# A decoder block's first stage in a written order, and a sink as a key column

## The chip, the cores and the metric

The kernel runs on one core of a Trainium2 chip. The metric is the device time of one execution in microseconds (us); the time of a kernel is the median of several runs.

## The reference

One residual block on x, 512 tokens by 1024 channels, in float32:

```python
h = rmsnorm(x, norm_mix)                     # x * rsqrt(mean(x*x) + eps) * g
proj = h @ w_in                              # split: qa, ka, va | qb, kc, vc, ksl, vsl, kw, vw, g_nsa | g_a, g_b
y_a = swa_sink_attention(qa, ka, va, sinks, table_a)      # 8 heads of 64, 2 key groups, window 128
y_b = nsa_attention(qb, compress(kc), compress(vc), ksl, vsl, kw, vw, sigmoid(g_nsa), table_b)
merged = sigmoid(g_a) * (y_a @ w_up_a) + sigmoid(g_b) * (y_b @ w_up_b)
x = x + merged @ w_out
u, g = split(causal_dwconv(rmsnorm(x, norm_ffn) @ w_ffn_in))
x = x + (silu(g) * u) @ w_ffn_out
out = rmsnorm(x, norm_final)
```

Of the sliding-window attention these lines matter here. The sink is one more logit for each head, which takes part in the softmax and has no value:

```python
logits = einsum('bqgrd,bkgd->bgrqk', qb, kb) * scale + bias      # bias: a function of query - key
logits = where(valid, logits, NEG)                               # 256 keys for 128 queries, the window is 128
probs = softmax(concatenate([logits, sink_col], axis=-1), axis=-1)[..., :span]
out = einsum('bgrqk,bkgd->bqgrd', probs, vb)
```

## The kernel before

All of it is one function, `hybrid`, in which nested helpers issue the work; the order of an engine's instructions is the order of the code, as a scheduling layer with priorities has arranged it. Products run on TensorE in a 32-bit form with fewer mantissa bits (fp32r). Each operand is therefore split into a high part (a cast on ScalarE, L79) and a low part (source minus high, L80, on VectorE or for weights named in `POOLJ` on GpSimd), and each product is three: high by high, high by low, low by high (`three`, L90).

The first stage takes the four token tiles of x in turn (`norm_x`, L152): squares and their sum on ScalarE (L156), the sum of two halves on VectorE (L158), a power on GpSimd, a scaling by the reciprocal root and the weight row `gam` on VectorE (L161), transposition on TensorE (L144), and the split into `xTh` and `xTl`. `values` (L171) then makes the 408 columns of values and gates of a tile with 24 products of 128x408 on TensorE. The weights `wv` for it come in two halves, `wvr` 0 and 1, each split whole (`wvh`, `wvl`).

After it a generator, `filler` (L213), hands out projections as jobs, named in `AORD` and `GORD`: `p_ka`, `p_qa` four times, `p_kc` and so on, each 24 products of 128x512, each with a weight load on SP's queue. Attention units call for the next piece of a job whenever they would wait. `unit_a` (L475) is one tile of 128 queries of one key group of the sliding window. Its first step makes four score tiles (`scores`, L439): two products, then one VectorE instruction (L449) that adds the bias tile TA, writes Pa and keeps the least value. The sink joins in three VectorE lines (L491, L494, L496) and a fifth exponential. Its second step scales, transposes and multiplies by VA.

The bias tile is made from the table by `pg` (L421, three products with a one-hot matrix `og`), copied back into the second half of `og` on ScalarE (L422), written to DRAM 32 times over as `gdr` (L423), and read back as a Toeplitz tile by `toeplitz` (L426 to L429), for TA in four DMAs of 32 partitions.

Of the kernel before, what the change touches and what calls it, by code (L numbers as in the profile page):

```python
# [6 lines left out]
F32 = mybir.dt.float32  # L7
# [4 lines left out]
P = 128  # L12
# [37 lines left out]
def hybrid(tc, x, wv, wblk, w1, w2, wua, wub, wout, wfi, wfo, nmix, nffn, nfin, sinks, par, table, onehot, out):  # L50
# [9 lines left out]
    with es:  # L60
        C = es.enter_context(tc.tile_pool(name="const", bufs=1))
        SL = es.enter_context(tc.tile_pool(name="slots", bufs=1))
        WR = es.enter_context(tc.tile_pool(name="wring", bufs=3))
        SM = es.enter_context(tc.tile_pool(name="small", bufs=4))
# [12 lines left out]

        def split(hi, lo, src, eng=None):
            A.copy(hi, src)  # L79
            (eng or V).tensor_tensor(lo, src, f(hi), op=ALU.subtract)  # L80
# [22 lines left out]
        for h in range(2):  # L103
            sl = slice(h * 512, (h + 1) * 512)
            nc.sync.dma_start(xt[0][:, sl], x[0:P, sl])
            if h == 0:
                nc.sync.dma_start(grow[:, :D], nmix)
        ones = grow[:, D:]
        V.memset(ones, 1.0)
        gam = [bank("sc", f"gam{h}") for h in range(2)]  # L110
        for h in range(2):
            T.matmul(gam[h], ones, grow[:, h * 512 : (h + 1) * 512], start=True, stop=True)
# [3 lines left out]
        nc.sync.dma_start(wvr[0], wv[0])  # L116
        nc.sync.dma_start(xt[1], x[P : 2 * P])
        nc.sync.dma_start(wvr[1], wv[1])
        for t in range(2, NT):
            nc.sync.dma_start(xt[t], x[t * P : (t + 1) * P])  # L120

        ident = C.tile([P, P], F32, name="ident")
        make_identity(nc, ident)
        mhalf = C.tile([P, 1], F32, name="mhalf")
        V.memset(mhalf, -0.5)
        prm = C.tile([P, par.shape[1]], F32, name="prm")
        nc.sync.dma_start(prm, par)
# [6 lines left out]
        def rstd_of(ssq, name):  # L134
            r = SM.tile([P, 1], F32, tag="rstd", name=f"rstd_{name}")
# [14 lines left out]
        halves = [slice(0, 512), slice(512, 1024)]  # L150

        def norm_x(t):  # L152
            s2 = SM.tile([P, 2], F32, tag="s2", name=f"s2x_{t}")
            for h in range(2):
                junk = bank("o", f"junk{t}{h}")
                A.activation(junk, xt[t][:, halves[h]], AF.Square, accum_out=s2[:, h : h + 1])  # L156
            ssq = SM.tile([P, 1], F32, tag="ssq", name=f"ssq{t}")
            V.tensor_tensor(ssq, s2[:, 0:1], s2[:, 1:2], op=ALU.add)  # L158
            r = rstd_of(ssq, f"n1_{t}")
            for h in range(2):  # L160
                V.scalar_tensor_tensor(xt[t][:, halves[h]], xt[t][:, halves[h]], r, gam[h], op0=ALU.mult, op1=ALU.mult)  # L161
                transposed(xt[t], xTh, xTl, t, h, "x")

# [7 lines left out]
        def values(t):  # L171
            ps = bank("mm", f"v{t}")
            sl = slice(t * P, (t + 1) * P)
            order = [(i, k) for h in range(2) for i in (0, 2) for k in range(4 * h, 4 * h + 4)] + [(1, k) for k in range(KD)]
            for n, (i, k) in enumerate(order):
                h, kk = k // 4, k % 4
                T.matmul(ps[:, :NV], (xh, xh, xl)[i](k)[:, sl], (wvh, wvl, wvh)[i][h][:, kk], start=(n == 0), stop=(n == 23))
# [12 lines left out]
        for h in range(2):  # L190
# [22 lines left out]
        def filler():  # L213
            i, nxt = 0, jobs[0][1]()
            while nxt is not None:
                name, _, run = jobs[i]
                cur, nxt, i = nxt, None, i + 1
                if i < len(jobs):
                    with hp(i >= HPJ):
# [96 lines left out]
        def keys(tile_, c0=0):  # L316
            def evac(ps):
                for g in range(2):
                    src = ps[64 * g : 64 * g + 64]
                    hi, lo = tile_()[:, g, 0, c0 : c0 + S], tile_()[:, g, 1, c0 : c0 + S]  # L320
# [24 lines left out]
        KA = lazy("KA", 6, [P, 2, 2, S])  # L345
# [12 lines left out]
        evacs = dict(kc=blocks_of(0), vc=blocks_of(1), ka=keys(KA), ksl=keys(KS, 32), kw=keys(KW),  # L358
# [47 lines left out]
        nsink = C.tile([P, 8], F32, name="nsink")  # L406
        nc.sync.dma_start(nsink, bc(sinks, 8))
        V.tensor_scalar(nsink, nsink, -1.0, None, op0=ALU.mult)
        tab = C.tile([33, 16], F32, name="tab")
        G.memset(tab, 1.0)  # L410
        nc.sync.dma_start(tab[:32], table)
        og = slot(15, [33, 2, ZA + ZW], F32, "og")
        oh, gsb = og[:, 0], og[:8, 1]
        nc.sync.dma_start(oh, onehot)
# [4 lines left out]
        for c0, c1, h0 in ((0, ZA, 0), (ZA, ZA + 512, 8), (ZA + 512, ZA + ZW, 8)):  # L419
            pg = bank("sc", f"pg{c0}")  # L420
            T.matmul(pg[:8, : c1 - c0], tab[:, h0 : h0 + 8], oh[:, c0:c1], start=True, stop=True)  # L421
            A.copy(gsb[:, c0:c1], pg[:8, : c1 - c0])  # L422
# [12 lines left out]
        TA = slot(10, [P, 8, 256], F32, "TA")  # L435
        toeplitz(TA, 0, 8, 0, 256)

# [37 lines left out]
        def unit_a(b, g):  # L475
            n = P if b == 0 else 256
            c0, y0 = (0, P) if b == 0 else ((b - 1) * P, 0)
            st = {}

            def s1():  # L480
                nm = SM.tile([P, 4], F32, tag="nma", name="nma", bufs=3)
                sm = SM.tile([P, 4], F32, tag="sma", name="sma", bufs=3)
                es_ = SM.tile([P, 4], F32, tag="esa", name="esa", bufs=3)
                pr = []
                for r in range(4):
                    p = AT.tile([P, 512], F32, tag="P", name="Pa", bufs=8)
                    c = scores(p, QA[g](), r, b, KA(), g, c0, n, TA, 4 * g + r, y0, nm[:, r : r + 1])
# [13 lines left out]
            def s2():  # L501
# [22 lines left out]
        def unit_b(b, g, br, st):  # L524
# [4 lines left out]
            def s1():  # L529
                Q, Tt = QB[g](), TB[g]  # L530
                nm = SM.tile([P, 4], F32, tag="nmb", name="nmb")
                sm = SM.tile([P, 4], F32, tag="smb", name="smb")
# [3 lines left out]
                if br == 1:  # L536
                    nc_, sc_ = (SM.tile([P, 4], F32, tag=t_, name=t_) for t_ in ("nmc", "smc"))
# [178 lines left out]
        for t in range(NT):  # L716
# [6 lines left out]
            s2 = SM.tile([P, 2], F32, tag="s2", name=f"s2_{t}")  # L723
# [5 lines left out]
            ssq = SM.tile([P, 1], F32, tag="ssq", name=f"ssq2_{t}")  # L729
# [34 lines left out]
        s2s = [SM.tile([P, 2], F32, tag=f"s3_{t}", name=f"s3_{t}", bufs=1) for t in range(NT)]  # L764
# [9 lines left out]
        for h in range(2):  # L774
# [10 lines left out]
            for t in range(NT):  # L785
# [13 lines left out]
                for c in range(2):  # L799
                    sl = slice(512 + 256 * c, 768 + 256 * c)  # L800
                    V.tensor_tensor(xo[:, sl], xo[:, sl], po[t][:, 256 * c : 256 * c + 256], op=ALU.add)
                    sc = SM.tile([P, 1], F32, tag="ssq", name=f"ssq3_{t}{c}")
                    A.activation(junk[:, sl], xo[:, sl], AF.Square, accum_out=sc)
                    V.scalar_tensor_tensor(ms, sc, 1.0 / D, ms, op0=ALU.mult, op1=ALU.add)
                r = SM.tile([P, 1], F32, tag="rstd", name=f"rstd_n3_{t}")
# [71 lines left out]
```

## Time and profile before

| | us |
|---|---|
| median of 3 runs | 770.8 (770.65 to 771.38) |
| the profiled execution | 771.21 |
| its span | 769.4 |
| TensorE busy | 747.5 (97%) |
| VectorE busy | 451.0 (59%) |
| ScalarE busy | 369.4 (48%) |
| GpSimd busy | 156.8 (20%) |
| mean granted TensorE clock | 0.989 |

The span is the time between the first and the last instruction of the profiled execution. PE is TensorE, DVE is VectorE, ACT is ScalarE, POOL is GpSimd, and SP issues DMAs. An entry `[3.67 <-DVE QB L333]` says how long an engine was idle just before an instruction, and what released it. The line numbers are those of the code above.

### The profile page before, as it was taken

The numbers are of one execution on the slowest core, as the hardware profiler recorded it, in microseconds if no ns is written. First come the engines' busy times: TensorE is split into PE (matmuls) and PEld (weight loads), VectorE is DVE, ScalarE is ACT, GpSimd is POOL, SyncE is SP. The second block draws the span as 40 slices with busy tenths as digits, with TensorE's granted clock in tenths as the row PEclk, the third lists the DMA queues.
The fourth block names the chain that finished last, engine by engine and source line by source line (L and its number), as shares of the span: only waits on it lengthen the run. The fifth ranks groups of instructions, "written<-read, shape, count | busy, mean of one in ns | idle before, by whom it ended". The sixth has DMA issues, their size and how long they took to land.

```text
span 769.4 us, 9745 instructions
## 1 busy us (share of the span) xinstructions
PE 747.5 (97%) x3590; PEld 623.3 (81%) x3590; DVE 451.0 (59%) x921; ACT 369.4 (48%) x692; POOL 156.8 (20%) x134
## 2 busy tenths in 40 slices
PE   7999989999999999999999999999999999999996
PEld 5788778788888888878889888888888888888885
DVE  5537988747655578759465665665556564214123
ACT  7345685745655856665344434343434443113213
POOL 5023536325333444402400000000000000002001
PEclk9999998999999999999999999999999999999999
DMA  8463335421112112405321323232322324232302
GB/s 304 98 148 111 108 93 169 126 83 55 56 55 83 55 60 69 145 1 192 111 78 60 109 83 110 82 110 89 104 92 101 102 90 136 85 107 85 107 28 109
DMA packets 24182, 76.74 MB, mean 100 GB/s; under 512 B 3748, under 2 KB 4900, under 8 KB 24134
## 3 DMA queue, kind: packets, MB, share of 16 engines
q1 hardware_dynamic: 24134, 76.12, 31.2%
q8 instruction: 28, 0.46, 0.3%
q14 instruction: 20, 0.16, 0.1%
HBM read 72.96 MB, written 3.15 MB: 99 GB/s over the span
## 4 chain that ended last, share of the span: by engine, by line
PE 89%; DVE 6%; issue 1%; POOL 1%; ACT 1%; DMA 1%; SPq 0%; POOLq 0%; DVEq 0%; ACTq 0%
PE ug L91 10%; PE ug L92 10%; PE ug L93 10%; PE fo L772 5%; PE fo L771 5%; PE fo L770 5%; PE pT L456 3%; PE up L91 2%; PE p_gb L91 2%; PE p_gb L92 2%; PE p_gb L93 2%; PE up L93 2%; PE up L92 2%; PE wo L91 2%; PE wo L92 2%; PE wo L93 2%
## 5 line engine op out<-in xcount | busy, mean ns | idle before, releaser
L92 PE MATMUL ug<-hTl,hl_fi 128*128 128x512 f32 (+1 forms) x376 | 141.1, 375 | 0.0
L93 PE MATMUL ug<-hTh,hl_fi 128*128 128x512 f32 (+1 forms) x376 | 141.1, 375 | 0.0
L91 PE MATMUL ug<-hTh,hl_fi 128*128 128x512 f32 (+1 forms) x376 | 140.9, 376 | 0.0
L93 PEld LDWEIGHTS ug<-hTh,hl_fi 128*128 128x128 f32 x376 | 70.8, 188 | 12.9
L91 PEld LDWEIGHTS ug<-hTh,hl_fi 128*128 128x128 f32 x376 | 70.6, 188 | 12.9
L92 PEld LDWEIGHTS ug<-hTl,hl_fi 128*128 128x128 f32 x376 | 70.8, 188 | 12.6
L754 ACT ACTIVATE cv<-ug,prm 128x512 f32<-128x512 f32 x44 | 34.3, 780 | 96.2 <-PE ug L93 96.2
L755 DVE SCALAR_TENSOR_TENSOR cv<-ug,prm,cv 128x511 f32<-128x511 f32 x44 | 33.0, 750 | 77.1 <-ACT cv L754 77.0
L771 PE MATMUL fo<-hl_fo,AH 128*128 128x512 f32 x176 | 68.8, 391 | 0.0
L770 PE MATMUL fo<-hl_fo,AH 128*128 128x512 f32 x176 | 67.3, 389 | 0.0
L796 POOL TENSOR_TENSOR X<-X,nfin 128x512 f32<-128x512 f32 x4 | 5.2, 1319 | 297.0 <-ACT junk L794 297.0
L80 DVE TENSOR_TENSOR hl_fo<-raw_fo,hl_fo 128x1024 fp32r<-128x1024 f32 x22 | 27.1, 1235 | 64.7 <-ACT hl_fo L79 64.7
L79 ACT CAST hl_fo<-raw_fo 128x1024 fp32r<-128x1024 f32 x22 | 23.1, 1052 | 65.8 <-PE fo L772 65.8
L80 DVE TENSOR_TENSOR hl_fi<-raw_fi,hl_fi 128x1024 fp32r<-128x1024 f32 x44 | 53.5, 1217 | 1.8 <-ACT hl_fi L79 1.8
L772 PE MATMUL fo<-hl_fo,AL 128*128 128x512 f32 x128 | 49.8, 389 | 0.0
L80 DVE TENSOR_TENSOR ptl<-pT,pth 128x512 fp32r<-128x512 f32 x54 | 36.5, 685 | 19.0 <-ACT pth L79 9.9
L378 ACT ACTIVATE Pb<-Pb,nmb 128x512 f32<-128x512 f32 (+3 forms) x64 | 35.9, 562 | 23.9 <-DVE nmb L449 23.6
L79 ACT CAST hl_fi<-raw_fi 128x1024 fp32r<-128x1024 f32 x44 | 45.5, 1037 | 2.4 <-PE wo L93 2.4
L79 ACT CAST pth<-pT 128x512 fp32r<-128x512 f32 x54 | 30.9, 587 | 17.7 <-PE ob L611 8.2
L771 PEld LDWEIGHTS fo<-hl_fo,AH 128*128 128x128 f32 x176 | 33.0, 188 | 7.2
L770 PEld LDWEIGHTS fo<-hl_fo,AH 128*128 128x128 f32 x176 | 33.0, 188 | 7.1
L449 DVE CUSTOM_DVE_ANT_0 Pb<-scores,TB 128x512 f32<-128x512 f32 (+3 forms) x64 | 30.7, 486 | 11.1 <-PE scores L445 9.2
(313 smaller groups left out, 1730.0 us busy)
## 6 DMA issues: line engine op xcount, KB each, us to landing
raw_fi<-in_wfi_dram SPq DMA_DIRECT2D x44, 512.0 KB, 3.3
raw_fo<-in_wfo_dram SPq DMA_DIRECT2D x22, 512.0 KB, 3.3
raw_w<-in_w_dram SPq DMA_DIRECT2D x8, 512.0 KB, 3.8
raw_ga<-in_wblk_dram SPq DMA_DIRECT2D x8, 512.0 KB, 3.3
raw_gb<-in_wblk_dram SPq DMA_DIRECT2D x8, 512.0 KB, 3.2
raw_wo<-in_wout_dram SPq DMA_DIRECT2D x5, 512.0 KB, 3.9
raw_qa<-in_wblk_dram SPq DMA_DIRECT2D x4, 512.0 KB, 4.9
raw_qb<-in_wblk_dram SPq DMA_DIRECT2D x4, 512.0 KB, 6.2
```

The lines of the kernel that those rows point to most:

```text
L79: A.copy(hi, src)
L80: (eng or V).tensor_tensor(lo, src, f(hi), op=ALU.subtract)
L91: T.matmul(ps, wh, xh, start=start, stop=False)
L92: T.matmul(ps, wh, xl, start=False, stop=False)
L93: T.matmul(ps, wl, xh, start=False, stop=stop)
L378: last_exp[0] = A.activation(a[0], a[1], AF.Exp, **k)
L449: V.tensor_tensor_reduce(ptile[:, :n], ps[:, :n], Tt[:, h, y0 : y0 + n], 1.0, HUGE, ALU.add, ALU.min, nm)
L754: A.activation(c, ps, AF.Identity, scale=cw(2, blk), bias=cb(blk))
L755: V.scalar_tensor_tensor(c[:, 1:], ps[:, : S - 1], cw(1, blk), c[:, 1:], op0=ALU.mult, op1=ALU.add)
L770: T.matmul(po[t], ah, wh, start=(k == 0), stop=False)
L771: T.matmul(po[t], ah, wl, start=False, stop=False)
L772: T.matmul(po[t], al, wh, start=False, stop=(k == NF - 1))
```

## The change

Four things are altered. **The first stage** is written out by hand, in a block whose order the scheduling layer keeps. x of tile 1 is loaded before the weights `wv`; the norm's row goes through ScalarE's queue; eight products on a zeroed tile (`busy`) stand ahead of the first work; each half of `wv` is split in two parts, and all low parts are made on GpSimd; the squares of a tile are summed and scaled by two VectorE operations; the products of different tiles are interleaved; the `pg` products and the copies of `og` stand late in the block. Weight loads of the projections are ordered behind the last transposed tile on their engines only. **GpSimd's subtractions** of a split (L80 before, L87 after) are cut into pieces of 256 columns. **The sink** becomes a column of keys: KA has two zero columns ahead of each tile of 128 keys, TA has two columns in its middle, one with the negative sink and one with 1e30, and the scores are 130 or 258 columns wide in place of 128 or 256; the sink's own lines go. TA is read back in two halves, eight DMAs. **The small tiles** are placed before the slots, with fewer buffers and sizes padded.

```diff
         def split(hi, lo, src, eng=None):
-            A.copy(hi, src)
-            (eng or V).tensor_tensor(lo, src, f(hi), op=ALU.subtract)
+            xparts.append(A.copy(hi, src))
+            step = 256 if eng is G else 1 << 20
+            n = hi.shape[-1]
+            for c in range(0, n, step):
+                sl = (slice(None),) * (len(hi.shape) - 1) + (slice(c, min(c + step, n)),)
+                xparts.append((eng or V).tensor_tensor(lo[sl], src[sl], f(hi)[sl], op=ALU.subtract))
...
-        norm_x(0)
-        VA = slot(16, [P, NT, 2, P], F32R, "VA")
-        for h in range(2):
-            split(wvh[h], wvl[h], wvr[h], (G, None)[h])
-        for t in range(1, NT):
-            norm_x(t)
-            values(t - 1)
-        values(NT - 1)
+        with tc.manual_schedule():
...
+            nc.scalar.dma_start(grow[:, :D], nmix)
...
+            busy(5)
...
+            busy(3)
+            squares(0)
+            squares(1)
+            scaled(0, 0)
+            scaled(0, 1)
+            wv_hi(0, 0)
+            x_T(0, 0)
...
+            values_out(1)
+            for c0, c1, h0 in ((0, ZA, 0), (ZA, ZA + 512, 8), (ZA + 512, ZA + ZW, 8)):
+                pg = bank("pt", f"pg{c0}")
+                T.matmul(pg[:8, : c1 - c0], tab[:, h0 : h0 + 8], oh[:, c0:c1], start=True, stop=True)
+                A.copy(gsb[:, c0:c1], pg[:8, : c1 - c0])
+            values(2, 1, (0, 2, 1))
...
         def filler():
-            i, nxt = 0, jobs[0][1]()
+            with tc.issue_after(xlast[0].ins), tc.issue_after(xlast[1].ins):
+                i, nxt = 0, jobs[0][1]()
...
-        TA = slot(10, [P, 8, 256], F32, "TA")
-        toeplitz(TA, 0, 8, 0, 256)
+        TA = slot(10, [P, 2112], F32, "TA")[:, :2064].rearrange("p (h y) -> p h y", h=8)
+        V.tensor_scalar(TA[:, :, P], nsink, -1.0, None, op0=ALU.mult)
+        V.memset(TA[:, :, P + 1], 1e30)
+        toeplitz(TA[:, :, :P], 0, 8, 0, P)
+        toeplitz(TA[:, :, P + 2 :], 0, 8, P, P)
...
-            n = P if b == 0 else 256
-            c0, y0 = (0, P) if b == 0 else ((b - 1) * P, 0)
+            n, nk, y0 = (P + 2, 1, P) if b == 0 else (2 * P + 2, 2, 0)
+            c0 = 0 if b == 0 else (b - 1) * (P + 2) + 2
...
-                ns = nsink[:, 4 * g : 4 * g + 4]
-                V.tensor_tensor(nm, nm, ns, op=ALU.min)
                 for r in range(4):
                     exp(pr[r][:, :n], pr[r][:, :n], bias=nm[:, r : r + 1], scale=-1.0, accum_out=sm[:, r : r + 1])
-                V.tensor_tensor(es_, nm, ns, op=ALU.subtract)
-                exp(es_, es_)
-                V.tensor_tensor(sm, sm, es_, op=ALU.add)
                 V.reciprocal(sm, sm)
```

On VectorE the first rows of the stage move. `ssq` is a tile's sum of squares, `x` the scaled tile, `xTl` its low part. Before, the scaling of the first tile's halves follows its own sum:

```order
L158 TENSOR_TENSOR ssq_120<-s2x_115 128x1
L136 TENSOR_SCALAR rstd_n_0_122<-ssq_120 128x1
L161 SCALAR_TENSOR_TENSOR x_79<-x_79,rstd_n_0_122,gam_85 128x512
L161 SCALAR_TENSOR_TENSOR x_79<-x_79,rstd_n_0_122,gam_86 128x512
L80 TENSOR_TENSOR xTl_111<-tp_x_0_126,xTh_109 128x4x128
L80 TENSOR_TENSOR xTl_112<-tp_x_1_134,xTh_110 128x4x128
```

and after, at the same place:

```order
L158 TENSOR_SCALAR ssq_146<-s2x_141 128x1
L159 TENSOR_SCALAR ssq_146<-s2x_141,ssq_146 128x1
L158 TENSOR_SCALAR ssq_156<-s2x_151 128x1
L159 TENSOR_SCALAR ssq_156<-s2x_151,ssq_156 128x1
L164 SCALAR_TENSOR_TENSOR x_75<-x_75,rstd_n_0_149,gam_131 128x512
L164 SCALAR_TENSOR_TENSOR x_75<-x_75,rstd_n_0_149,gam_132 128x512
L87 TENSOR_TENSOR xTl_92<-tp_x_0_164,xTh_90 128x4x128
```

The sums of the second tile (`ssq_156`) now stand ahead of the scaling of the first.

On ScalarE the middle of the stage has squares (`junk`), weight casts (`wvh`) and the high parts `xTh`. Before:

```order
L79 CAST wvh_91<-wvr_89 128x1632
L79 CAST xTh_109<-tp_x_0_126 128x4x128
L156 ACTIVATE junk_147,s2x_146<-x_79 128x512
L79 CAST xTh_110<-tp_x_1_134 128x4x128
L156 ACTIVATE junk_149,s2x_146<-x_79 128x512
L79 CAST wvh_92<-wvr_90 128x1632
L156 ACTIVATE junk_207,s2x_206<-x_80 128x512
L156 ACTIVATE junk_209,s2x_206<-x_80 128x512
```

and after, from the first part of `wvh`:

```order
L170 CAST wvh_83<-wvr_81 128x816
L81 CAST xTh_90<-tp_x_0_164 128x4x128
L81 CAST xTh_91<-tp_x_1_172 128x4x128
L170 CAST wvh_83<-wvr_81 128x816
L81 CAST xTh_90<-tp_x_0_192 128x4x128
L156 ACTIVATE junk_200,s2x_199<-x_76 128x512
L156 ACTIVATE junk_202,s2x_199<-x_76 128x512
L170 CAST wvh_84<-wvr_82 128x816
L81 CAST xTh_91<-tp_x_1_211 128x4x128
L170 CAST wvh_84<-wvr_82 128x816
```

The squares of the third tile stand between the second tile's first `xTh` and the cast of the second weight half.

Further on, still on ScalarE, are the copies of the bias rows `og`, behind which the write of `gdr` is issued. `hl_ka` and `hl_qa` are weights of the first projections, `eg` a tile's gates. Before:

```order
L79 CAST hl_qa_368<-raw_qa_366 128x1024
L79 CAST xTh_109<-tp_x_0_217 128x4x128
L422 COPY og<-pg_418 8x384
L79 CAST hl_qa_435<-raw_qa_433 128x1024
L182 ACTIVATE eg_201<-v_172 128x24
L422 COPY og<-pg_421 8x512
L79 CAST xTh_110<-tp_x_1_225 128x4x128
L422 COPY og<-pg_424 8x128
```

and after:

```order
L81 CAST xTh_91<-tp_x_1_305 128x4x128
L81 CAST VA<-v_227 128x2x64
L81 CAST hl_ka<-raw_ka 128x1024
L81 CAST hl_qa_410<-raw_qa_408 128x1024
L81 CAST hl_qa_467<-raw_qa_465 128x1024
L81 CAST VB<-v_227 128x4x64
L192 ACTIVATE eg_329<-v_227 128x24
L274 COPY og<-pg_333 8x384
L274 COPY og<-pg_336 8x512
L274 COPY og<-pg_339 8x128
```

The copies stood among the third tile's `xTh` and now follow the fourth tile's last `xTh`, the weight casts and the values of the second tile.

## Rows read from the trace of the kernel before

**Rows 1.** The page: busy time, share of the span, instructions by engine.

```profile
PE 747.5 (97%) x3590; PEld 623.3 (81%) x3590; DVE 451.0 (59%) x921; ACT 369.4 (48%) x692; POOL 156.8 (20%) x134
```

**Rows 2.** Waits of TensorE: waiter, releaser, us in all, count, us each.

```profile
PE h L275 <- DVE QB L333: 3.7, 1, 3.7
...
PE p_ga L91 <- DVE KW L324: 1.2, 1, 1.2
PE p_ksl L91 <- DVE cx L260: 1.0, 1, 1.0
```

**Rows 3.** Timeline of 109.9 to 115.9 us: start, duration, engine, line, operation.

```profile
109.95 2.38 POOL L80 TENSOR_TENSOR hl_w<-raw_w,hl_w 128x1024 fp32r<-128x1024 f32 x1
...
110.77 1.58 DVE L491 TENSOR_TENSOR nma<-nma,nsink 128x4 f32<-128x4 f32 x1
...
112.29 2.35 POOL L80 TENSOR_TENSOR hl_qb<-raw_qb,hl_qb 128x1024 fp32r<-128x1024 f32 x1
112.38 2.27 DVE L494 TENSOR_TENSOR esa<-nma,nsink 128x4 f32<-128x4 f32 x1
...
115.52 0.55 PE L275 MATMUL h<-hl_w,XX 128*128 128x256 f32 x1 [3.67 <-DVE QB L333]
```

**Rows 4.** VectorE by line, 55 to 125 us: busy, mean ns, idle before.

```profile
L494 DVE TENSOR_TENSOR esa<-nma,nsink 128x4 f32<-128x4 f32 x7 | 5.8, 828 | 0.1
...
L496 DVE TENSOR_TENSOR sma<-sma,esa 128x4 f32<-128x4 f32 x7 | 1.1, 160 | 1.7 <-ACT esa L378 1.7
```

**Rows 5.** Windows: length; busy PE, PEld, DVE, ACT, POOL; granted clock; DMA share, GB/s.

```profile
90.84:94.25 3.41, 3.41 (x10) 2.64 (x9) 3.38 (x7) 1.83 (x4) 2.75 (x2) 0.50 0.42 154
114.73:121.56 6.83, 6.04 (x20) 5.23 (x21) 5.58 (x19) 2.60 (x7) 3.18 (x3) 0.50 0.96 306
```

**Rows 6.** Timeline of TensorE in the first stage.

```profile
18.73 0.60 PE L144 MATMUL tp_x<-ident,x 128*128 128x128 f32 x4
...
37.22 1.66 PE L177 MATMUL v<-wvl,xTh 128*128 128x408 f32 x8
38.71 0.40 PE L91 MATMUL p_ka<-xTh,hl_ka 128*128 128x512 f32 x1
```

**Rows 7.** Timeline of ScalarE in the first stage.

```profile
5.30 0.60 ACT L156 ACTIVATE junk<-x 128x512 f32<-128x512 f32 x1 [1.13 <-DMA x<-in_x_dram]
...
7.32 1.55 ACT L79 CAST wvh<-wvr 128x1632 fp32r<-128x1632 f32 x1 [1.30 <-DMA wvr<-in_wv_dram]
...
9.04 0.59 ACT L79 CAST xTh<-tp_x 128x512 fp32r<-128x512 f32 x1 [0.16 <-PE tp_x L144]
...
22.22 1.04 ACT L79 CAST hl_qa<-raw_qa 128x1024 fp32r<-128x1024 f32 x1
...
26.64 0.25 ACT L422 COPY og<-pg 8x128 f32<-8x128 f32 x1 [2.30 <-PE pg L421]
```

**Rows 8.** Timeline of VectorE in the first stage.

```profile
7.08 1.41 DVE L161 SCALAR_TENSOR_TENSOR x<-x,rstd_n,gam 128x512 f32<-128x512 f32 x2 [0.68 <-PE gam L112]
...
24.79 1.21 DVE L80 TENSOR_TENSOR hl_qa<-raw_qa,hl_qa 128x1024 fp32r<-128x1024 f32 x1
```

**Rows 9.** Timeline of SP's queue: DMA issues.

```profile
10.73 0.30 SPq L414 DMA_DIRECT2D og<-in_onehot_dram  x1
...
26.92 0.31 SPq L423 DMA_DIRECT2D gdr<-og  x1
...
48.65 1.89 SPq L429 DMA_DIRECT2D TA<-gdr  x4
```

**Rows 10.** Timeline of the first bias addition and what follows it.

```profile
56.28 0.29 DVE L449 CUSTOM_DVE_ANT_0 Pa<-scores,TA 128x128 f32<-128x128 f32 x1 [3.56 <-DMA TA<-gdr]
...
57.95 0.69 DVE L333 SCALAR_TENSOR_TENSOR QA<-p_qa,QA 64x512 fp32r<-64x512 f32 x1 [0.33 <-ACT QA L332]
...
61.65 0.45 PE L91 MATMUL p_qa<-xTh,hl_qa 128*128 128x512 f32 x1
```

More of the change, by code (lines that the diff above doesn't have):

```diff
@@ L102, in hybrid @@
         xt = [(x01, x23)[t // 2][:, t % 2] for t in range(NT)]
-        for h in range(2):
[L104 to L107, printed above, removed]
+        halves = [slice(0, 512), slice(512, 1024)]
+        grow = slot(6, [1, D + P], F32, "grow")
         ones = grow[:, D:]
[L109 to L112, printed above, removed]
+        og = slot(15, [33, 2, ZA + ZW], F32, "og")
+        oh, gsb = og[:, 0], og[:8, 1]
+        tab = SM.tile([33, 16], F32, tag="tab", name="tab", bufs=1)
+        nsink = SM.tile([P, 8], F32, tag="n8", name="nsink", bufs=1)
         wvr = [slot(7 + h, [P, 4, NV], F32, f"wvr{h}") for h in range(2)]
@@ L115, in hybrid @@
         wvl = [slot(11 + h, [P, 4, NV], F32R, f"wvl{h}") for h in range(2)]
[L116 to L120, printed above, removed]
+        warm = C.tile([P, 2], F32, name="warm")
+        mhalf = warm[:, 1:2]
         ident = C.tile([P, P], F32, name="ident")
-        make_identity(nc, ident)
-        mhalf = C.tile([P, 1], F32, name="mhalf")
-        V.memset(mhalf, -0.5)
         prm = C.tile([P, par.shape[1]], F32, name="prm")
-        nc.sync.dma_start(prm, par)
         cw = lambda tap, blk: prm[:, tap * 44 + blk : tap * 44 + blk + 1]
@@ L134, in rstd_of @@
         def rstd_of(ssq, name):
-            r = SM.tile([P, 1], F32, tag="rstd", name=f"rstd_{name}")
+            r = SM.tile([P, 1], F32, tag="rstd", bufs=3, name=f"rstd_{name}")
             V.tensor_scalar(r, ssq, 1.0 / D, EPS, op0=ALU.mult, op1=ALU.add)
@@ L149, in hybrid @@
         xTl = [slot(2 + h, [P, 4, S], F32R, f"xTl{h}") for h in range(2)]
[L150 to L162, printed above, removed]
         xh = lambda k: xTh[k // 4][:, k % 4]
@@ L169, in hybrid, with squares, scaled, x_T @@
         gate = C.tile([P, NT, 3, 8], F32, name="gate")
-        def values(t):
-            ps = bank("mm", f"v{t}")
-            sl = slice(t * P, (t + 1) * P)
[L174 to L177, printed above, removed]
+        VA = slot(16, [P, NT, 2, P], F32R, "VA")
+        st_x, st_v = {}, {}
+        def squares(t):
+            s2 = SM.tile([P, 2], F32, tag="s2", bufs=3, name=f"s2x_{t}")
+            for h in range(2):
+                junk = bank("o", f"junk{t}{h}")
+                A.activation(junk, xt[t][:, halves[h]], AF.Square, accum_out=s2[:, h : h + 1])
+            m = SM.tile([P, 1], F32, tag="ssq", bufs=3, name=f"ssq{t}")
+            V.tensor_scalar(m, s2[:, 0:1], 1.0 / D, EPS, op0=ALU.mult, op1=ALU.add)
+            V.tensor_scalar(m, s2[:, 1:2], 1.0 / D, m, op0=ALU.mult, op1=ALU.add)
+            st_x[t] = SM.tile([P, 1], F32, tag="rstd", bufs=3, name=f"rstd_n1_{t}")
+            G.tensor_tensor(st_x[t], m, mhalf, op=ALU.pow)
+        def scaled(t, h):
+            V.scalar_tensor_tensor(xt[t][:, halves[h]], xt[t][:, halves[h]], st_x[t], gam[h], op0=ALU.mult, op1=ALU.mult)
+        def x_T(t, h):
+            transposed(xt[t], xTh, xTl, t, h, "x")
+        def wv_hi(h, c):
+            A.copy(wvh[h][:, 2 * c : 2 * c + 2], wvr[h][:, 2 * c : 2 * c + 2])
+        def wv_lo(h, c):
+            cs = slice(2 * c, 2 * c + 2)
+            G.tensor_tensor(wvl[h][:, cs], wvr[h][:, cs], f(wvh[h])[:, cs], op=ALU.subtract)
+        def values(t, h, parts):
+            if t not in st_v:
+                st_v[t] = bank("mm", f"v{t}")
+            sl = slice(t * P, (t + 1) * P)
+            for i in parts:
+                for k in range(4 * h, 4 * h + 4):
+                    T.matmul(st_v[t][:, :NV], (xh, xh, xl)[i](k)[:, sl], (wvh, wvl, wvh)[i][h][:, k % 4],
+                             start=(h == 0 and i == 0 and k == 0), stop=(h == 1 and i == 1 and k == 7))
+        def values_out(t):
+            ps = st_v[t]
             pv = ps[:, 0:384].rearrange("p (n d) -> p n d", d=64)
@@ L218, in filler @@
                 if i < len(jobs):
-                    with hp(i >= HPJ):
+                    with hp(i >= HPJ), tc.issue_after(xlast[0].ins), tc.issue_after(xlast[1].ins):
                         nxt = jobs[i][1]()
@@ L343, in lazy, with ka @@
             return get
-        KA = lazy("KA", 6, [P, 2, 2, S])
+        def ka():
+            if "KA" not in made:
+                made["KA"] = slot(6, [P, 2112], F32R, "KA")[:, :2080].rearrange("p (g l b k) -> p g l b k", g=2, l=2, b=NT)
+                G.memset(f(made["KA"])[:, :, :, :, 0:2], 0.0)
+            return made["KA"]
+        KA = ka
         KS = lazy("KS", 7, [P, 2, 2, 32 + S])
@@ L418, in hybrid @@
         gdr = DR.tile([COPIES, 8, ZA + ZW], F32, name="gdr")
[L419 to L422, printed above, removed]
         nc.sync.dma_start(gdr.rearrange("c h z -> h c z"), gsb[:, None, :].to_broadcast([8, COPIES, ZA + ZW]))
@@ L536, in s1 @@
                 if br == 1:
-                    nc_, sc_ = (SM.tile([P, 4], F32, tag=t_, name=t_) for t_ in ("nmc", "smc"))
+                    nc_, sc_ = (SM.tile([P, 4], F32, tag=t_, name=t_, bufs=2) for t_ in ("nmc", "smc"))
                     pcs = mine["pcs"] = AT.tile([P, 4, 32], F32, tag="pcs", name="pcs")
@@ L763, in hybrid @@
         nc.sync.dma_start(NFN, bc(nfin, D))
-        s2s = [SM.tile([P, 2], F32, tag=f"s3_{t}", name=f"s3_{t}", bufs=1) for t in range(NT)]
+        s3 = SM.tile([P, 8], F32, tag="n8", name="s3", bufs=1)
+        s2s = [s3[:, 2 * t : 2 * t + 2] for t in range(NT)]
         def fo_mm(po, t, hl, kk, k):
```

113 lines of the change are left out of this document (83 added, 30 removed).

## The prediction

> **What bounds the kernel now.** I read the page's busy shares first, then what ends TensorE's waits, then the two stretches in which it stands or runs slowly, then the first 60 us by engine. The profiled execution took 771.21 us with a span of 769.4, and the runs shown have a median of 770.8, so the sum is made against 771.2 and the median is taken 0.4 lower. TensorE is busy for 747.5 of 769.4 us [rows 1]: it is the bound, and an edit counts only where TensorE starts earlier or later, or runs at its lower clock. The change adds almost no products after the first stage (two more columns in 64 score products, at 0.45 us for 512 columns [rows 10] some 0.1 us in all). The worth of it lies in TensorE's stands.
>
> Three of them lie behind VectorE later on: 3.7 us before `h`, 1.2 before `p_ga` and 1.0 before `p_ksl` [rows 2]. The timeline shows how the first arises: L491 and L494, operations on 128x4 numbers, take 1.58 and 2.27 us, each lasting until near the end of a GpSimd subtraction of 2.4 us beside them [rows 3]. What QB's evacuation stands behind is therefore GpSimd's long subtraction. L494 has a mean of 828 ns, where L496, an addition of the same size that meets none, has 160 [rows 4]. [...]
>
> **The sink column and GpSimd's four pieces.** The change drops L491, L494, L496 and the exponential of `esa` from each of eight units, and cuts each GpSimd subtraction of 1024 columns into four, so that a waiting VectorE operation gets in after about 0.6 us. GpSimd's own time rises little (2.4 to some 2.5 us) and it is busy for 156.8 us [rows 1]; TensorE hides that. In the best case all comes back: 3.7 + 3.0 at 112, 1.0 + 1.7 at 90 and the 1.2 before `p_ga`, together 10.6. I take the first pair whole, since both VectorE operations of that chain are gone, and half of the other 3.9, whose waits are for evacuations that remain: **-8.7** (bounds -6.7 and -10.6).
>
> **The first stage.** TensorE's needs in it are 32 transposes (0.15 us each [rows 6]), 96 value products (0.187 us each: eight from 37.22 to 38.71 [rows 6]) and three small ones. What sets its pace is how ScalarE and VectorE serve it, and both run their rows in the written order. I followed the four queues by hand, with the durations of before for each row, and 0.05 us a handoff. Landings: x1 now stands ahead of wv0, whose landing ScalarE saw at 7.3 [rows 7]. With 0.5 MB to wv0's 0.8 I put x1 at 6.6, wv0 at 8.6 and wv1 at 10.7, as now: `og`'s load, behind it in the queue's slots, is issued at 10.73 [rows 9].
> The squares of x1 (two of 0.6 with their accumulator reads, 1.5 together [rows 7]) end at 8.1; VectorE has both their sums ahead of the scaling of x0, which thus starts at 8.4 and not at 7.08 [rows 8]. Transposes 9.2, xTh (0.59 [rows 7]) 9.9 and 10.6, half a wv cast (half of 1.55 [rows 7], and 0.1) each at 8.7 and 11.0, products from 10.6. Then ScalarE's order bites. xTh of x1 (13.8), then the squares of x2 (14.3 to 15.8), then the cast of wv1 (15.8 to 16.7), for which TensorE has stood since 14.2: 2.6 us. The squares of x3 (22.6 to 24.2) have their sums ahead of the scaling of x2's second half (24.4 to 25.1) on VectorE: TensorE stands from 22.7, 2.4 us. A third stand of 1.5 follows at 29.2, before the last transposes, and three of 0.8 to 1.0. Products for tile 2 start at 32.1; 48 x 0.187 and the `pg` products (1.0) put `p_ka` at **42.2**, where it was 38.71 [rows 6]: +3.5. If TensorE's clock falls after one such stand, as it did after those at 90 and 112, 1.7 to 3.0 come on top [rows 5]; none to two such falls are the bounds. One is taken, and since the longest stand will be the one of the next part, the larger row: +3.0. The eight zero products change only whether the first transposes run at the higher level: at the lower, another 1.1 us here.
>
> **The bias chain.** This is the term that decides. The bias rows `og` go to memory (`gdr`) and come back as the sliding window's bias tile TA. Before, the write is issued at 26.92 [rows 9], just behind the last `og` copy of ScalarE (26.64 [rows 7]); the TA loads are issued when it has landed, 21.7 us later, at 48.65 [rows 9], and the first bias addition starts at 56.28, having waited 3.56 us for TA [rows 10]. VectorE does that addition in turn, so QA's evacuation behind it comes at 57.95, and `p_qa2`, which needs that bank, starts at 61.65 [rows 10].
> After, the three `og` copies stand on ScalarE behind VA of tile 1 (32.4), three weight casts (1.04 each [rows 7], until 35.6) and VB and the gate of tile 1. VB and the gate wait in turn for VectorE, which has two weight subtractions of 1.21 [rows 8] before its part, until 37.4. The copies (0.47, 0.56, 0.25) end at 38.6: the write is **11.7 us** later. Its 21.7 us I keep (same bytes). TA then comes in eight DMAs of 512-byte pieces in place of four of 1024; the last four decide for tile 0. Four took 7.6 us [rows 9, 10]; by bytes eight take the same, by pieces twice that, 15.2. I take 9.3, near the former, as the halves of a piece move half the bytes: TA at 38.6 + 21.7 + 9.3 = 69.6. Behind it two evacuations, as 56.28 to 58.6 now [rows 10], so `p_qa2` at **72.0**. TensorE's own work (`p_ka` at 42.2, four projections at the present 5.7 us each, (61.65 - 38.71) / 4 [rows 6, 10]) would bring it there at 65, so the chain is later than TensorE, and the delay of the first stage lies inside it: **+10.35** against 61.65, not to be added to +3.5.
> On the split of TA a row bears: at present pieces of 1024 bytes land in 7.6 us. [...]
>
> **The rest.** The two sums per tile in place of one (0.15 us), the memsets of KA's and TA's columns and the moved parameter loads lie beside TensorE's work: nothing, or 0.3 us where they stand on VectorE's part of the chain above. The small tiles' pool and its 256-byte padding move addresses. The `oa` products read tiles that start off such a boundary before, at the pace of the projections: I take zero, with -1 and +1 as bounds. That the scores now stand in pairs closer together before `p_qa3` may cost 1.5 if their evacuation is late; I leave it in the range.
>
> **Sum.** +10.35 (bias chain) + 3.0 (clock after the long stand) - 8.7 = +4.7, so 771.2 + 4.7 = 775.9 profiled, 775.5 as a median. Forecast **775.5 us**; its own range is 771 to 780.
>
> **Rivals.**
> A, faster. The hand model of the first stage is too slow. If ScalarE and VectorE hand over faster, so that the stands of 2.6, 2.4 and 1.5 vanish and the `og` copies end at 32, TA is there at 63.0 and `p_qa2` starts at 65.4. The chain is then +3.7, the clock may fall once (+3.0), and all 10.6 and the bound of 1 for the addresses come back: 771.2 + 3.7 + 3.0 - 11.6 = 766.3. For it: the sum of TensorE's work is small, and weight loads have landed by then. Against: ScalarE's rows stand in a fixed order, and each duration is a row of before. With my other terms the sum is zero for a write at 34.
> B, no change: the chain is late by half of what I say (+5.2 + 3.0 - 8.7), or the clock does not fall and everything is given back (+10.35 - 10.6): 771.
> C, much slower: TA's eight DMAs take 15.2 us, so TensorE stands 6 us more, and the clock falls in two gaps of the first stage, while only 6.7 is given back: 771.2 + 10.35 + 6 + 3 + 1.7 - 6.7 = 785.5, or 781 with one term less. It decides as soon as pieces count and not bytes.
> D, the change doesn't do what it says: VectorE's stalls remain because another GpSimd operation, the 128x256 multiplications of Pa, blocks as well; then 6.7 of the gain fall away: 782, inside C.
>
> **Chances.** Forecast 0.42, A 0.28, B 0.13, C with D 0.17. What a measurement of this kernel can tell from no change is about 0.2%, 769.3 to 772.3: faster 0.31, within 0.13, slower 0.56. The range that leaves out 2 in 10 reaches from 764 (A with no fall of the clock: 771.2 + 3.7 - 10.6) to 784, the middle of C.
>
> **What would show it.** Right: TensorE stands for some 7 us before `p_qa2`, released by VectorE behind a TA wait; the `gdr` write is issued near 38; `h` after QB waits for less than 1 us, and VectorE's short operations no longer last 1.5 us beside GpSimd. Wrong: the write before 33, or no wait on TA at all; a first stage with less than 3 us of stands, `p_ka` before 38.

## The result and the profile after

The changed kernel takes 784.57 us (median of 4 runs, 783.08 to 785.51), the kernel before 771.09 beside it. The ratio is 1.0167, with a 95% interval of 1.0142 to 1.0193: slower, as forecast, but by 13.5 us where 4.7 were predicted, and above the range. The profiled execution took 785.51 us with a span of 783.5.

The page of the changed kernel, its first part (busy us, share, instructions), answers to [rows 1]:

```profile
PE 752.9 (96%) x3598; PEld 626.2 (80%) x3598; DVE 424.2 (54%) x898; ACT 368.9 (47%) x686; POOL 183.1 (23%) x258
```

TensorE is busy for 5.4 us more, VectorE for 26.8 less, and GpSimd for 26.3 more: it makes all low parts of `wv` now, and four pieces cost it 2.8 us where one operation took 2.4 [rows 3], not the 2.5 that the prediction had. What TensorE waits for (waiter, releaser, us in all, times, longest), to be held against [rows 2]:

```profile
PE scores L530 <- DVE QA L422: 5.9, 2, 5.2
PE tp_x L136 <- DVE x L164: 4.5, 3, 2.3
PE p_kw L98 <- DVE cx L366: 3.2, 1, 3.2
PE v L183 <- ACT wvh L170: 2.7, 3, 2.0
...
PE h L360 <- DVE cx L366: 0.2, 1, 0.2
```

The stand of 3.7 us before `h` is gone. In its place stand one of 5.2 before a score behind QA's evacuation, a new one of 3.2 before `p_kw`, and 7.2 us in the first stage (4.5 before transposes, 2.7 before value products). There, on TensorE's timeline (start, duration, what ended the idle time before):

```profile
1.64 2.50 PE L224 MATMUL idle<-VA 128*128 128x512 f32 x5 [1.64 <-DVE VA L204]
...
10.27 1.97 PE L136 MATMUL tp_x<-ident,x 128*128 128x128 f32 x8 [0.84 <-DVE x L164]
...
19.75 1.05 PE L183 MATMUL v<-wvh,xTh 128*128 128x408 f32 x2 [1.95 <-ACT wvh L170]
21.00 1.05 PE L183 MATMUL v<-wvh,xTh 128*128 128x408 f32 x2 [0.21 <-ACT wvh L170]
21.85 1.56 PE L183 MATMUL v<-wvh,xTl 128*128 128x408 f32 x4
...
26.50 0.60 PE L136 MATMUL tp_x<-ident,x 128*128 128x128 f32 x4
...
30.14 0.63 PE L136 MATMUL tp_x<-ident,x 128*128 128x128 f32 x4 [2.29 <-DVE x L164]
...
35.65 0.63 PE L136 MATMUL tp_x<-ident,x 128*128 128x128 f32 x4 [1.40 <-DVE x L164]
...
37.69 0.90 PE L183 MATMUL v<-wvh,xTl 128*128 128x408 f32 x4
...
47.90 0.40 PE L98 MATMUL p_ka<-xTh,hl_ka 128*128 128x512 f32 x1
```

Four products of one shape last 1.56 us at 21.85 and 0.90 at 37.69. By that pace TensorE is at its lower level until 25.53, where the trace's first record of the granted clock, 1.00, begins; in the trace of the kernel before, the first record is at 12.33. `p_ka` starts 9.2 us later than before. Then the bias chain, on ScalarE, on SP's queue, on VectorE and on TensorE:

```profile
27.62 0.61 ACT L156 ACTIVATE junk<-x 128x512 f32<-128x512 f32 x1
...
37.15 0.28 ACT L81 CAST VA<-v 128x128 fp32r<-128x128 f32 x1
...
43.01 0.19 ACT L192 ACTIVATE eg<-v 128x24 f32<-128x24 f32 x1 [2.46 <-DVE VB L87]
43.10 1.08 ACT L274 COPY og<-pg 8x384 f32<-8x384 f32 x3
```

```profile
44.21 0.31 SPq L506 DMA_DIRECT2D gdr<-og  x1
66.75 3.79 SPq L512 DMA_DIRECT2D TA<-gdr  x8
```

```profile
74.79 0.29 DVE L535 CUSTOM_DVE_ANT_0 Pa<-scores,TA 128x130 f32<-128x130 f32 x1 [12.89 <-DMA TA<-gdr]
```

```profile
75.86 0.47 PE L530 MATMUL scores<-KA,QA 128*128 128x130 f32 x1 [5.22 <-DVE QA L422]
...
77.70 0.73 PE L98 MATMUL p_qa<-xTh,hl_qa 128*128 128x512 f32 x1
```

On ScalarE the first row is the squares of the fourth tile and the second VA of the second tile; the `og` copies stand behind the gate `eg`, which had waited 2.46 us for VB on VectorE. VectorE waits 12.89 us for TA (3.56 before [rows 10]), QA's evacuations stand behind it, and `p_qa2` starts at 77.70 in place of 61.65. Behind the stand the granted clock is 0.50, with 7.03 us of busy PE in the stretch (length; busy PE, PEld, DVE, ACT, POOL; clock, DMA share, GB/s), as in [rows 5]:

```profile
75.86:83.55 7.69, 7.03 (x18) 5.59 (x19) 6.79 (x18) 4.02 (x9) 3.92 (x7) 0.50 0.36 136
```

At 0.50 the products run at little more than half the pace. Those of `p_qa2` start 0.43 us apart in this stretch and 0.23 behind it; in the trace of the kernel before, those of `p_ksl` do the same in the first stretch of [rows 5], which ends at 94.25, and behind it:

```profile
92.69 0.63 PE L91 MATMUL p_ksl<-xTh,hl_ksl 128*128 128x512 f32 x1
93.12 0.63 PE L92 MATMUL p_ksl<-xTl,hl_ksl 128*128 128x512 f32 x1
...
94.80 0.39 PE L91 MATMUL p_ksl<-xTh,hl_ksl 128*128 128x512 f32 x1
95.03 0.39 PE L92 MATMUL p_ksl<-xTl,hl_ksl 128*128 128x512 f32 x1
```

### The profile page after: what moved, and what is told of

It reads as the page before. It is cut to its first block, busy times and chain, and to the rows that moved or that the text cites. A ratio compares the mean times of both kernels' runs of the same rounds, so it can differ in the third digit from the quotient of the medians.

```text
span 783.5 us, 9911 instructions
## 1 busy us (share of the span) xinstructions
PE 752.9 (96%) x3598; PEld 626.2 (80%) x3598; DVE 424.2 (54%) x898; ACT 368.9 (47%) x686; POOL 183.1 (23%) x258
## 4 chain that ended last, share of the span: by engine, by line
PE 79%; DMA 7%; ACT 6%; DVE 4%; issue 2%; POOL 1%; SPq 1%; POOLq 0%; DVEq 0%; ACTq 0%
PE ug L100 10%; PE ug L99 10%; PE ug L98 10%; PE fo L852 5%; PE fo L853 5%; PE fo L854 5%; DMA gdr<-og 3%; PE pT L542 2%; PE p_ga L98 2%; PE p_ga L99 2%; PE p_ga L100 2%; PE wo L100 1%; PE wo L99 1%; PE wo L98 1%; PE scores L530 1%
## 5 line engine op out<-in xcount | busy, mean ns | idle before, releaser
L87 DVE TENSOR_TENSOR hl_fo<-raw_fo,hl_fo 128x1024 fp32r<-128x1024 f32 x22 | 27.1, 1235 | 64.6 <-ACT hl_fo L81 64.6
L87 DVE TENSOR_TENSOR hl_fi<-raw_fi,hl_fi 128x1024 fp32r<-128x1024 f32 x44 | 53.5, 1217 | 0.8 <-ACT hl_fi L81 0.6
L87 DVE TENSOR_TENSOR ptl<-pT,pth 128x512 fp32r<-128x512 f32 x54 | 36.6, 684 | 15.4 <-ACT pth L81 9.9
```

The lines of the kernel that those rows point to most:

```text
L87: xparts.append((eng or V).tensor_tensor(lo[sl], src[sl], f(hi)[sl], op=ALU.subtract))
```

## The experiments

The theory: the late bias write makes the loss, through the wait on TA and the clock behind it. The rival: the slower first stage makes it, and slack behind would absorb a late TA. The others divide what is lost in the first stage and what the rest gives back. A ratio is to the kernel before on the same chip. That kernel's median lay between 771.1 and 773.5 us on the chips used, so kernels from different chips are compared by their ratios; a time in the text is the median, a start in the text is from the profiled execution.

**Early bias write.** The `pg` loop is moved up in the written order:

```diff
             values(0, 1, (0, 2))
+            for c0, c1, h0 in ((0, ZA, 0), (ZA, ZA + 512, 8), (ZA + 512, ZA + ZW, 8)):
+                ...
             values(1, 0, (0, 2))
...
             values_out(1)
-            for c0, c1, h0 in ((0, ZA, 0), (ZA, ZA + 512, 8), (ZA + 512, ZA + ZW, 8)):
-                ...
```

> The changed kernel with the three pg products and the og copies moved ahead, behind tile 0's second set of products. Theory (the late bias write is what costs): the write of gdr is issued near 26 us in place of 44.2, TA is there near 57, VectorE no longer waits for it, p_qa2 starts at 70.7 (61.65 + 9.2, what p_ka is late) in place of 77.7, and the clock does not fall at 73. That is -7.0 and -3.5: 774 to 776 us. Rival (the first stage alone costs, and later slack hides the wait on TA): 782 or more.

779.2 us, 1.0088 (1.0055 to 1.0120). The wait on TA and the fall of the clock behind it are gone, yet the time is 2 to 4 us above the expectation (1.0088 of 771.2 is 778.0): in the profiled execution the level fell again twice inside the first stage, from 21.15 to 31.39 and from 34.80 to 38.22, and `p_ka` started at 53.42. From there on the kernel goes as expected: `p_ka` is 14.7 us later than in the kernel before and the last product 9.0; in the changed kernel these are 9.2 and 14.1. The late write thus costs (14.1 - 9.2) - (9.0 - 14.7) = 10.6 us, for 10.5 expected. The new stage is no smaller matter: without the late write this kernel is still 1.0088 of the one before, where the same kernel with the old stage (next experiment but one) is 0.9884.

**Late bias write, old first stage.** The kernel with the first stage of before and all else of the change (the next experiment), and one order edge:

```diff
+        with tc.issue_after(last_p[-1].ins):            # the last value product
             for c0, c1, h0 in ((0, ZA, 0), (ZA, ZA + 512, 8), (ZA + 512, ZA + ZW, 8)):
```

> The kernel with the old first stage (764.2), with one edit: the pg products wait for the last value product, so that og's copies and the write of gdr come 15 to 25 us later, and nothing else of the stage moves. Theory (the late write alone makes most of the loss): TA is there 30.5 us after the write (22.5 and 8.0), p_qa2 starts 2.9 behind that, and the time is 764.2 plus its lateness against 60.5 plus 3.5 of clock: 780 for a write at 43, 785 for one at 48. Rival (a late TA is absorbed by slack behind it): below 770.

783.99 us, 1.0154 (1.0120 to 1.0189), where the same kernel without the edge takes 764.18 (0.9884). The write is issued at 47.44 (25.83 without the edge), and:

```profile
76.74 0.29 DVE L473 CUSTOM_DVE_ANT_0 Pa<-scores,TA 128x130 f32<-128x130 f32 x1 [22.93 <-DMA TA<-gdr]
```

```profile
77.81 0.48 PE L468 MATMUL scores<-KA,QA 128*128 128x130 f32 x1 [15.55 <-DVE QA L346]
...
79.65 0.73 PE L100 MATMUL p_qa<-xTh,hl_qa 128*128 128x512 f32 x1
```

`p_ka` starts at 39.15, nearly where it did before (38.71), and yet a loss as large as that of the whole change is there. Against the kernel without the edge the write is 21.6 us later, `p_qa2` 19.05 and the last product 21.9. So some 2.6 us were absorbed ahead of `p_qa2`, and the rival is out: nothing behind it absorbs a late TA.

**Old first stage, the rest of the change**, against the changed kernel:

```diff
-        with tc.manual_schedule():
-            ...
+        norm_x(0)
+        ...                      # as in the kernel before, pg and og after need("ka")
```

> The first stage, its loads and the pg products as in the kernel before, with everything else of the change (GpSimd's four pieces, the sink as a key column, TA in eight DMAs, the small tiles' pool). Theory (the rest of the change gives back some 5 to 9 us, the new first stage loses 20): 762 to 766 us, no wait of h on QB. Rival (the rest gives nothing, since other waits take the place of those that go): 769 to 772.

764.18 us, 0.9884 (0.9862 to 0.9907). The rest of the change gives back about 9 us (7.2 to 10.6 by the interval; 6.5 at the last product in the traces), and the new first stage loses it and 13 more. What TensorE waits for in this kernel:

```profile
PE gam L119 <- DMA grow<-in_nmix_dram: 3.3, 1, 3.3
PE p_kw L98 <- DVE cx L288: 2.7, 1, 2.7
...
PE h L282 <- DVE cx L288: 0.2, 1, 0.2
```

**GpSimd's pieces alone**, in the kernel before:

```diff
+            step = 256 if eng is G else 1 << 20
```

> The kernel before with GpSimd's subtractions in four pieces of 256 columns, and nothing else. If the length of GpSimd's operations is what holds VectorE, L491 and L494 last under 1 us near 112, the stand before h and the fall of the clock behind it go: 764 to 766 us. If the VectorE lines of the sink have to go as well, 769 to 771.

766.61 us, 0.9914 (0.9894 to 0.9934): most of the gain. The two VectorE lines are still there, and by line (busy, mean ns, idle before) last less than half of what they did: 349 ns for 828 [rows 4], and 241 for the 514 of L491 before:

```profile
L501 DVE TENSOR_TENSOR esa<-nma,nsink 128x4 f32<-128x4 f32 x7 | 2.4, 349 | 0.2
L498 DVE TENSOR_TENSOR nma<-nma,nsink 128x4 f32<-128x4 f32 x7 | 1.7, 241 | 0.1
```

`h`'s wait for QB falls to 1.1 us. The granted clock no longer falls near 91 or 115; one fall is left, of 3.41 us at 123.13.

**The sink column alone**: the old first stage, the column, `split` as before.

> The kernel before with the sink as a key column (and TA in eight DMAs, the small tiles' pool), GpSimd's subtractions whole. If taking L491 and L494 away is enough, the stand of 3.7 us before h goes: 764 to 767 us. If the next VectorE operation with two operands in its place meets GpSimd's 2.4 us as they did: 768 to 771.

769.58 us, 0.9978 (0.9959 to 0.9996): the stand before `h` goes (0.8 us left, in two), and 2.6 before `p_kw` and 1.6 before `oa` behind VectorE take most of its place. By the ratios, whose intervals lie apart, taking the blocked lines away gains less than shortening what blocks them. The two traces do not show that: counted from the start of `p_kc`, this one gains 3.4 us on the kernel before and that with the pieces 3.6 (both edits together: 5.5). This one is already 1.7 us late there, behind a first stage whose rows the edit doesn't reorder, so the size of the difference stays open.

**Ones, and no early products.** Two edits of the changed kernel:

```diff
-            V.memset(f(zero), 0.0)
+            V.memset(f(zero), 1.0)
```

> The changed kernel with the zeroed tile of the eight early products filled with ones instead. Theory (products of zeros do not bring TensorE's clock up, products of other numbers would): the higher level is recorded before 12 us in place of 25.5, the first stage's products run at 0.19 us in place of 0.34, p_ka starts near 43 in place of 47.9, the whole kernel takes about 779 us. Rival (the stands between the products of the first stage keep the clock low, whatever the early products multiply): the record stays at 25.5 and the time within 1 us of 784.6.

785.22 us, 1.0155 (1.0139 to 1.0170), the higher level first recorded at 23.07, `p_ka` at 48.20. And without `busy(5)` and `busy(3)`:

> The changed kernel without the eight early products. If products ahead of the data do nothing for the clock of what follows, p_ka starts within 1 us of 47.9 and the time is within 1 us of 784.6 (gam's products end some 2 us earlier, which nothing waits for). If the eight bring the clock up even a little earlier, the level rises later than 25.5 and the time goes up by 1 to 3 us.

782.46 us, 1.0148 (1.0128 to 1.0168), the higher level at 16.62 and again, after a fall, at 23.44, and `p_ka` at 46.51, 1.4 us earlier than with them. No gain from the early products could be measured, with zeros or ones; that the kernel without them is 2 us faster (1.5 by the ratios) lies within what the intervals leave open.

**Filled stands.** The early write, and products into a bank that nobody reads, in four stands:

```diff
             x_T(1, 1)
+            pad(5)               # wvh by xTh, 128x408
...
+            pad(8)
             x_T(2, 1)
...
+            pad(5)
             x_T(3, 1)
+            pad(3)
             values(2, 0, (0, 2, 1))
```

> The kernel with the early pg products (779.2), and in four stands of the first stage products whose result is thrown away (a weight by x, as the real ones: 5, 8, 5 and 3 of 128x408). Theory (the stands between products keep the clock at its lower level): the level rises by 18 and does not fall again in the stage, p_ka starts near 43 to 45, although 21 products more are done, and the time is 768 to 771 us. Rival (the stage is paced by ScalarE and VectorE, the clock matters little): p_ka at 48 or later, 775 us or more.

774.77 us, 1.0054 (1.0034 to 1.0073), where the kernel without the fill has 1.0088; the intervals overlap. The level rises at 16.89, before the first of these products (17.14), so they did not raise it; but it never falls again, where without them it fell at 21.15, behind the stand that the first five now fill. `p_ka` starts at 47.77, 5.65 us earlier than without the fill, but later than the 43 to 45 expected. Both theories were partly right. The transposes of the third tile's second half, `x_T(2, 1)`, start at 30.07 for 34.23: that is the clock. But they still stand for 0.8 us behind a scaling on VectorE, the next ones for 0.5, and value products for 1.4, 0.6 and 1.7 behind ScalarE: that is the rows' order.

**Squares earlier**, on the early write: `squares(2)` and `squares(3)` right behind `wv_hi(0, 1)`.

```diff
             wv_hi(0, 1)
+            squares(2)
+            squares(3)
```

> The kernel with the early pg products (779.2), and besides the squares of the third and fourth tile moved up in the written order, to where ScalarE stood idle from 13.6 to 16.9 us. Theory (the place of these squares in ScalarE's row makes TensorE stand before the value products of wv1, before the second half of the third tile and of the fourth): the stands of 2.0, 2.1 and 1.4 us go, x_T of the third tile's second half starts right behind its first, p_ka at 42 to 44, or 3 to 5 later if the clock falls in the stage; the time is 5.75 less than 771.2 plus the lateness of p_ka: 769 to 771. Rival (the stage is paced by the clock alone): p_ka stays at 47 or later, 775 or more.

776.14 us, 1.0064 (1.0042 to 1.0086). The stand of 2.0 us falls to 0.6, but two of 1.4 stay: there the scaling stands in VectorE's row behind a low part that waits for ScalarE. `p_ka` is at 46.80, with the level low until 22.29 and once more from 35.94 to 39.35.

**Scalings earlier too**, without and with six products in two of the stands that are left:

```diff
             x_T(1, 1)
+            pad(3)               # in the second kernel only, and 3 before values(2, 0)
+            scaled(2, 0)
+            scaled(2, 1)
+            scaled(3, 0)
+            scaled(3, 1)
```

> The kernel with the early squares and pg products (776.1), and the four scalings of the third and fourth tile moved up in VectorE's row too, ahead of the low parts of the third tile's transposes. Theory (with the squares early, the stands of 1.4 us before the transposes come from VectorE's row, where a scaling stands behind a low part that waits for ScalarE): those two stands go, p_ka starts 2.5 to 3 us earlier, near 44, and the time is 773 to 774. Rival (what is left of p_ka's lateness is the clock's lower level alone): no stand, but p_ka at 46 or later since the level rises later; 776.

> The same, and three products whose result is thrown away in each of two stands that stay (before the value products of wv1, and before those of the third tile). Theory (stands keep the clock down): the level rises by 18 and stays, p_ka at 40 to 42, 767 to 769 us. Rival (the level rises when it does, whatever stands there): as the run without them within 1 us.

773.88 us, 1.0016 (0.9992 to 1.0040), and 770.87, 0.9988 (0.9970 to 1.0006). In the first, both stands of 1.4 are gone, `p_ka` starts at 44.17 as expected, and what remains, beside 2.1 us in four short ones, is:

```profile
PE v L183 <- ACT eg L192: 3.2, 2, 1.7
```

The second comes out 3.0 us faster, with intervals that overlap by a little, and less than expected (767 to 769): the level rises at 19.64 (21.89 without the six) and not by 18, and `p_ka` is at 43.19. In the two traces the last products come the other way round (761.17 without, 762.16 with), and the level does not fall inside the stage in either, so a gain of the six products is not shown. The whole kernel is then even with the one before: `p_ka` is still 4.5 us later than there, and the rest of the change makes it up.

**Further on the best.** In the kernel with the old stage, `p_kw` stands for 2.7 us, and its weights land 8.3 us after their issue, behind four loads of TB. Two of those four are put behind the weights:

```diff
-            toeplitz(TB[g], 4 * g, 4, ZA, 512)
+            if g:
+                toeplitz(TB[g], 4 * g, 4, ZA, 512)
...
+            if not g:
+                need("kw")
+                toeplitz(TB[g], 4 * g, 4, ZA, 512)
```

> The kernel with the old first stage (764.2), in which two of the four loads of the next bias tile TB are issued behind the weights of p_kw in place of ahead of them. There the weights took 8.3 us to land, and p_kw's stand of 2.7 us follows. If the queue is the cause, the weights land about 3 us earlier and the stand goes: 761 to 763 us. If what p_kw waits for is VectorE's own work, no change: 764.

763.01 us, 0.9896 (0.9870 to 0.9922), the stand at 1.1. The intervals of the two overlap, and the ratio is no lower than 0.9884: that the stand shrinks is shown, a gain in time is not. The traces say why it drowns. From the start of `p_kc` on this one gains 6.9 us on the kernel before, for 5.5, but `p_ka` is at 40.30 for 37.60, behind a first stage with the same instructions, in which the level is low again from 21.71 to 28.54 in this trace and stays up in the other. And the norm's row through ScalarE's queue:

> The kernel with TB's loads behind p_kw's weights (763.0), with the norm's row loaded through ScalarE's queue as the change does it. gam's products wait 3.3 us for that row now and scale x at 7.08. If gam bounds the start, x is scaled near 6.3 and the time is 0.5 to 1 lower, 762 to 763; if the squares do, no change, or 0.5 more for the issue on ScalarE.

762.12 us, 0.9864 (0.9832 to 0.9895): `gam` waits 2.5 us and not 3.3, and x is scaled at 5.95 for 7.12, but `p_ka` is at 40.23 for 40.30: what is won at the start does not reach it. The time can't be told from 763.01. It is the lowest ratio measured here, though its interval overlaps that of 0.9884.

## Why the prediction was wrong

The direction and the chain were right. The sum of three terms was 9.6 us short of the profiled execution (+4.7 for +14.3): 5.7 in the bias chain, 3.4 in what comes back, 0.5 in the clock behind the stand. The 5.7 come for the most part from the first stage, and there the step failed.

- **The first stage.** The step that failed is the one on the zero products: they "change only whether the first transposes run at the higher level: at the lower, another 1.1 us here". The hand model ran every value product at 0.187 us, the pace of the higher level, and the level came at 25.53. The rows show where 5.7 us went. The first transposes are 1.1 late (10.27 for 9.2; x1's squares begin at 7.82, where x1 was put at 6.6), the products of `wv1` 2.95 (19.75 for 16.8), the squares of the fourth tile 5.0 (27.62 for 22.6), and `p_ka` 5.7 (47.90 for 42.2). About 1.1 of this is x1's landing, some 4 fall where products and transposes run at half pace, and 0.7 came later; this split is an estimate from these rows. That the lower level costs such time is shown by the early write without and with the fill, which have the same products between the first of `wv1` and the third tile's transposes: 10.84 us with the level low from 21.15, 6.74 with it high. The stands that the prediction had named are all there, by place and releaser: 2.0, 2.3 and 1.4 us for 2.6, 2.4 and 1.5. That they come from the rows' order is shown (squares and scalings earlier: the stands go, the ratio falls from 1.0088 to 1.0016).
- **The bias chain** was +10.35 and is +16.05. The write is 5.6 late (44.21 for 38.6), since the `og` copies stand behind all of that stage on ScalarE: the cast of VA for the second tile ends at 37.43 for 32.4, which is 5.0 of it; the weight casts behind it won 0.3 back. A further 0.9 is a cost that the prediction had left out: the two weight subtractions on VectorE, for which VB and the gate wait, took 3.28 us beside GpSimd's pieces, and were put at 2 x 1.21. The links behind the write hold: 22.5 us of write for 21.7, and TA in 8.0 for 9.3. TA's eight loads, in pieces of 512 bytes, took 8.0 us, where four in pieces of 1024 took 7.6 for the same bytes: 0.4 more, and the 15.2 by pieces did not come.
- **The clock behind the long stand** was +3.0 and is 7.03 / 2 = 3.5. Like the 1.7 and 3.0 at 90 and 112, half of the 3.41 and 6.04 us busy in [rows 5], it is an estimate from the busy time at 0.50, where a product takes 0.43 us for the 0.23 at 1.00.
- **What comes back** was -8.7; the sum leaves 14.3 - 16.05 - 3.5 = -5.3. With the old first stage the kernel is 1.1 us ahead of the one before at `p_kc`'s end and 6.6 at the last product, so -5.5 there too. Row by row, 3.5 before `h`, 1.2 before `p_ga` and both falls of the clock (1.7 and 3.0) did come back. Against them stand 3.2 before `p_kw` (2.7 with the old stage), behind TB's loads, 0.8 before `p_qb`, 0.5 before `oa` and 0.2 more before `p_ksl`. The prediction had no such term: it gave a stall back without asking what was late next. That -8.7 was too much is shown by single traces only; by the ratio with the old stage, 7.2 to 10.6 us come back, some of it perhaps in the first stage.
- **Rival C** had the right time, 785.5, by luck: its reason was TA by pieces, 15.2 us, and TA took 8.0. Rival A (a stage faster than by hand) was the opposite of what came. D is out, since the stand before `h` is gone (0.2 us left).

What stays open: why the level rises so late in the new stage. In the eight kernels with it the first record of the higher level lies between 16.6 and 25.5 us, in the seven with the old one between 12.3 and 15.5, and filled stands came with 16.9 and 19.6. But two kernels whose instructions are the same up to 22 us, the changed one and the one with the early write, differ by 7.8 us in it, so a single trace doesn't separate the cause.

## What to carry to other kernels

When a step is moved, follow the longest chain that hangs on it, a write to memory and back above all: here 31 us lie between a copy of 8 rows and the first use of the tile, and of the 21.6 us by which an order edge alone made the write late, 19.05 reached `p_qa2`, and nothing behind it made them up. In a written order, a row that belongs to a later tile (squares, scalings) must not stand ahead of one that the matrix engine already waits for, nor behind one that waits itself: here such rows made stands of 2.0, 2.3 and 1.4 us. And cut a long operation of one engine that keeps another off before taking the victims away: the pieces alone gave 0.9%, the removal of the blocked lines 0.2%. Such pieces have a price where they run beside the other engine's long operations, and here 0.9 us of it lay on the bias chain.

## What was not expected of the hardware

Eight products in a row, 7.8 us from 1.64 on with the gains' products between them, did not bring TensorE to its higher level, with zeros or with ones: the eight transposes behind them took 1.97 us, 0.25 each, where the higher level gives 0.15 [rows 6]. After it had risen, the level fell again inside the first stage in four of the eight kernels with the new stage (at 20.03, 21.15, 29.89 and 35.94) and in six of the seven with the old one (between 21.5 and 24.2). In the two kernels with filled stands it did not fall, but neither did it in two with open ones, the changed kernel and the one with early scalings, so that filling keeps it up is not shown. And GpSimd's pieces are not free of VectorE: beside two VectorE subtractions of 1024 columns, GpSimd's four pieces took 4.77 us and VectorE's two 3.28, against 2.82 alone and 2 x 1.21 [rows 8]:

```profile
38.47 4.77 POOL L87 TENSOR_TENSOR hl_ka<-raw_ka,hl_ka 128x256 fp32r<-128x256 f32 x4 [6.35 <-ACT hl_ka L81]
...
55.96 2.82 POOL L87 TENSOR_TENSOR hl_kc<-raw_kc,hl_kc 128x256 fp32r<-128x256 f32 x4 [9.89 <-ACT hl_kc L81]
```

```profile
39.37 3.28 DVE L87 TENSOR_TENSOR hl_qa<-raw_qa,hl_qa 128x1024 fp32r<-128x1024 f32 x2 [0.97 <-ACT hl_qa L81]
```
